# Weight blocks of the q and k projections placed 32 bytes apart, in eleven forms

## The chip, the cores and the metric

The kernel runs on one core of a Trainium2 chip. The metric is the device time of one execution in microseconds (us). The kernel before takes 675.37 us, the median of three runs (675.22, 675.37 and 675.39). A core has a matrix engine (TensorE, in the profile PE for its matmuls and PEld for its weight loads), a vector engine (VectorE, DVE), a scalar engine (ScalarE, ACT), a general engine (GpSimd, POOL) and a queue engine that issues DMAs (SyncE, SP).

## The reference: what is computed

A decoder trunk of two layers on 256 tokens of width 1024, everything in float32. Layer 0 mixes tokens with a forgetting attention of 16 heads of 64, layer 1 with a block attention that, at 256 tokens, is one causal block with a relative bias. After each mixer stands a SwiGLU of inner width 2816, and after it a gated embedding. Cut to what matters here:

```python
for i in range(DEPTH):                        # DEPTH = 2
    u = _rmsnorm(h, attn_norm_g[i])
    proj = u @ w_in[i]                        # 1024 x 3072: q, k and v
    q, k, v = heads(proj)                     # 16 heads of 64
    h = h + merge(attention_i(q, k, v)) @ w_o[i]
    u = _rmsnorm(h, ffn_norm_g[i])
    gu = u @ ffn_w_in[i]                      # 1024 x 5632
    h = h + (silu(gu[..., :D_FF]) * gu[..., D_FF:]) @ ffn_w_out[i]
    gate = sigmoid(_rmsnorm(h, ple_norm_g[i]) @ ple_w_gate[i])
    h = h + gate * (p[i] @ ple_w_up[i])
return _rmsnorm(h, final_norm_g)
```

## The kernel before, in words

**Weights.** All weights come as 216 *halves*, each 128 partitions by 1024 float32 columns (512 KB), in the order in which they are used. The function `half` takes the next one: SP issues its DMA into a buffer `raw`, ACT copies it, rounded, into a buffer `whi` (line 136), and DVE writes the difference of the two into `wlo` (line 137). There are six buffers each of `raw`, `whi` and `wlo`, so the three steps run ahead of the matmuls until a buffer that they need is still in use. The activations are split into a high and a low part in the same way (`nm.hi`, `nm.lo`), and every product is three matmuls (`mm3`, lines 82 to 84): high by high, high by low, low by high.

**Where a weight block lies.** The buffers are longer than the 1024 columns. `blocks` (which calls `half` with `at=APART`, 16 columns or 64 bytes) is used where the weights are the stationary operand of a matmul: each half is then eight blocks of 128 by 128, one for each step k of the sum over the width. `LINE` is 64 columns, 256 bytes. There is already one exception to an even placement: with `entry` (used for the first half of the SwiGLU's input weights that follows two output halves, and once for a half that comes after the matmuls of a norm), the low parts of the first two blocks begin 32 bytes (`FURTHER`, 8 columns) further than an even placement would have them, and the low parts of the other six 256 bytes further; DVE then writes `wlo` in two instructions (line 128), one of 256 and one of 768 columns. The high part stays in one piece, written by ACT at line 125.

**The attention stage.** First come eight halves for v, then sixteen for q and k. `project(j, a)` computes the queries (a = 0) or keys (a = 1) of the two heads of pair j: one half, eight blocks, 24 matmuls with 256 columns moving, into the tile `pq`. The work is written out in this order by hand, for j from 0 to 7:

```python
for j in range(NP):
    project(j, 0)
    if j >= 1:
        scores(j - 1)
    if j >= 2:
        transposes(j - 2)
    project(j, 1)
    if j >= 2:
        values(j - 2)
```

`scores` (tile `sp`) multiplies queries by keys and runs the softmax on DVE and ACT; it needs `qkt`, `qkh` and `qkl`, which DVE and ACT make from `pq` (lines 387 and 238). `transposes` (tile `pp`, line 429) turns the probabilities, `values` (tile `po`, lines 82 to 84 and 444) multiplies them by v. So from j = 2 on `project(j, 1)` follows transposes on TensorE, and from j = 3 on `project(j, 0)` follows values. `project(1, 1)` follows scores alone. The 24 matmuls of `project(2, 0)` come straight behind those of `project(1, 1)`.

What an engine executes is in one order that is fixed when the program is built, from the order in which the work is written and from when buffers come free; on each engine an instruction that waits holds up all that stand behind it. In a few places, therefore, the order on TensorE is not the written one: in layer 1 three matmuls of `project(3, 0)` stand among those of the first `values`.

**The other stages** that use `blocks` are the SwiGLU's input halves (tile `gu`, 24 matmuls each, as above). The output projection (`wo`), the SwiGLU's output (`fo`), v and the gate (`pg`) use the weights as the moving operand, 512 columns wide.

Of the kernel before, what the change touches and what calls it, by code (L numbers as in the profile page):

```python
# [28 lines left out]
F32R = mybir.dt.float32r  # L29
AF = mybir.ActivationFunctionType  # L30
ALU = mybir.AluOpType

P = 128
S = 256
D = 1024
KT = D // P
# [10 lines left out]
HW = 1024  # L47
# [7 lines left out]
LINE = 64  # L55
APART = 16
# [3 lines left out]
FURTHER = 8  # L60


@with_exitstack
def trunk(ctx: ExitStack, tc: tile.TileContext, x, xt, pt, w, wf, cst, gains, gf, bf, rel, hot, rvm, out):
    nc = tc.nc
    one = ctx.enter_context(tc.tile_pool(name="one", bufs=1))
    work = ctx.enter_context(tc.tile_pool(name="work", bufs=2))
# [4 lines left out]
    def bank(name):  # L72
        return ps.tile([P, 512], F32, tag="bank", name=name)

    def f32(ap):
        return ap.bitcast(F32)
# [3 lines left out]
    def mm3(o, a, b, start, stop):  # L80
        (ah, al), (bh, bl) = a, b
        mm(o, ah, bh, start=start, stop=False, skip_group_check=True)  # L82
        mm(o, ah, bl, start=False, stop=False, skip_group_check=True)  # L83
        mm(o, al, bh, start=False, stop=stop, skip_group_check=True)  # L84
# [26 lines left out]

    state = {"next": 0}

    def half(at=0, entry=0):


        i = state["next"]
        state["next"] += 1
        raw = work.tile([P, HW], F32, tag="raw", bufs=RAW, name=f"raw{i}")
        hi = work.tile([P, HW + LINE], F32R, tag="whi", bufs=6, name=f"whi{i}")[:, at:at + HW]  # L120
        lt = work.tile([P, HW + 2 * LINE], F32R, tag="wlo", bufs=6, name=f"wlo{i}")
        lo = lt[:, at:at + HW]
        if entry:
            nc.sync.dma_start(raw, w[i])
            nc.scalar.activation(hi, raw, AF.Copy)  # L125
            ats = [(at + FURTHER, 0, entry), (at + LINE, entry, HW)]
            for a, c0, c1 in ats:
                nc.vector.tensor_tensor(lt[:, a + c0:a + c1], raw[:, c0:c1], f32(hi[:, c0:c1]), op=ALU.subtract)  # L128
            return hi, [lt[:, a + k * P:a + (k + 1) * P] for a, c0, c1 in ats for k in range(c0 // P, c1 // P)]
        parts = 2 if i < 2 else 1  # L130
        for q in range(parts):
            c = slice(q * HW // parts, (q + 1) * HW // parts)
            if i == 0 and q == 1:
                nc.sync.dma_start(hx[:, 1], xt[:, 1])
            nc.sync.dma_start(raw[:, c], w[i][:, c])
            nc.scalar.activation(hi[:, c], raw[:, c], AF.Copy)  # L136
            nc.vector.tensor_tensor(lo[:, c], raw[:, c], f32(hi[:, c]), op=ALU.subtract)  # L137
        return hi, lo

    def blocks(entry=False):  # L140

        hi, lo = half(APART, ENTRY * P if entry else 0)
        hi = [hi[:, k * P:(k + 1) * P] for k in range(KT)]
        return hi, lo if entry else [lo[:, k * P:(k + 1) * P] for k in range(KT)]
# [54 lines left out]

    nm = Norm(0)  # L200
    first = [half()]
    nm.block(0, hx[:, 0])
    nm.block(1, hx[:, 1])
    first.append(half())
    for b in range(1, 4):
        nc.sync.dma_start(hx[:, 2 * b:2 * b + 2], xt[:, 2 * b:2 * b + 2])
# [14 lines left out]
    ht = work.tile([BUCKETS, RVW], F32, tag="e", bufs=3, name="ht")  # L221
# [14 lines left out]
    def split(hi, lo, src):  # L236
        nc.scalar.activation(hi, src, AF.Copy)  # L237
        nc.vector.tensor_tensor(lo, src, f32(hi), op=ALU.subtract)
# [86 lines left out]
    def attention(layer, nm, mid, early, nf):  # L325
        vb = [bank(f"v{layer}_{b}") for b in range(4)]
        rest = None
        for c in range(4):
            wt = [early.pop(0) if early else half() for _ in range(2)]
            for kk in range(2):  # L330
                hi, lo = wt[kk]
                k = 2 * c + kk
# [23 lines left out]
        for t in range(2):  # L356
            for hf in range(2):
                col = nm.col[:, t:t + 1]
                src = vb[2 * t + hf].rearrange("p (j s d) -> p j s d", s=2, d=DH)
                for s in range(2):  # L360
                    at = (slice(None), slice(4 * hf, 4 * hf + 4), slice(2 * s * DH, (2 * s + 1) * DH))
# [7 lines left out]
        o = work.tile([P, NP, 2, S], F32R, tag="act", name=f"o{layer}")  # L369
# [3 lines left out]
        pq = {}  # L373

        def project(j, a):
            hi, lo = blocks()
            if a == 0:
                pq[j] = bank(f"pq{layer}_{j}")
            bk = pq[j]
            for k in range(KT):  # L380
                mm3(bk[:, a * S:(a + 1) * S], (hi[k], lo[k]), nm.k(k),
                    start=(k == 0), stop=(k == KT - 1))
            if a == 0:
                return
            del pq[j]
            t = work.tile([P, 2, S], F32, tag="qkt", name=f"qkt{layer}_{j}")
            nc.vector.tensor_tensor(t.rearrange("p a s -> p (a s)"), bk,
                                    nm.row.rearrange("p a s -> p (a s)"), op=ALU.mult)
            th = work.tile([P, 2, S], F32R, tag="qkh", name=f"qkh{layer}_{j}")
            tl = work.tile([P, 2, S], F32R, tag="qkl", name=f"qkl{layer}_{j}")  # L390
            split(th, tl, t)
            qk[j] = t, th, tl
# [54 lines left out]
# [9 lines that stand above are left out]
            if layer == 0 and j >= 4:  # L456
                moba[0](j - 4)
# [23 lines left out]
    def ffn(layer, nm, filler, np_):  # L481
# [3 lines left out]
        def up(fs):  # L485

            bks = {f: bank(f"gu{layer}_{f}") for f in fs}

            def step(f, a, wt, k, start):
                mm3(bks[f][:, a * S:(a + 1) * S], (wt[0][k], wt[1][k]), nm.k(k), start, k == KT - 1)  # L490

            if fs[0] == 0:
                wts = {f: (blocks(), blocks()) for f in fs}
                for k in range(KT):
                    if k == 3:
                        nm.turn(1)
                        nm.square(1)
                    for f in fs:
                        for a in range(2):
                            step(f, a, wts[f][a], k, k == 0 and a == 0)  # L500
                nm.root()
                return fs, bks
            for a in range(2):
                wt = blocks(a == 1 if fs[0] == 2 else a == 0 and fs[0] % 2 == 0)
                for k in range(KT):
                    step(fs[0], a, wt, k, k == 0)
                if fs[0] == 2 and a == 0:
                    nm.spread()
                    gated(*early)
            gated(fs, bks)  # L510
# [154 lines left out]
    for layer in range(2):  # L665
# [5 lines left out]
        got = []  # L671
# [98 lines left out]
```

## Time and profile before

| | |
|---|---|
| median of three runs | 675.37 us |
| the profiled execution | 675.98 us, with a span of 674.2 us from its first to its last instruction |
| instructions | 11845 |
| PE busy | 658.9 us (98% of the span), 4604 matmuls |
| DVE busy | 455.1 us (67%) |
| ACT busy | 386.1 us (57%) |
| granted TensorE clock | 0.998 of full speed |

The profiled execution is thus 0.61 us longer than the median of the runs. In the profile's rows, L82 is line 82 of the kernel, `pq<-g,whi` says that tile `pq` is written from tiles `g` and `whi`; a group of like instructions has its busy time in us and the mean duration of one in ns, and then the idle time of the engine just before them with what ended it. In a list in order of time, the first column is the start in us from the span's start and the second the duration. Matmuls follow each other before the one before has ended, so the pace at which TensorE works is the distance between two starts, and not the duration of one.

### The profile page before, as it was taken

The numbers are of one execution on the slowest core, as the hardware profiler recorded it, in microseconds if no ns is written. First come the engines' busy times: TensorE is split into PE (matmuls) and PEld (weight loads), VectorE is DVE, ScalarE is ACT, GpSimd is POOL, SyncE is SP. The second block draws the span as 40 slices with busy tenths as digits, with TensorE's granted clock in tenths as the row PEclk, the third lists the DMA queues.
The fourth block names the chain that finished last, engine by engine and source line by source line (L and its number), as shares of the span: only waits on it lengthen the run. The fifth ranks groups of instructions, "written<-read, shape, count | busy, mean of one in ns | idle before, by whom it ended". The sixth has DMA issues, their size and how long they took to land.

```text
span 674.2 us, 11845 instructions
## 1 busy us (share of the span) xinstructions
PE 658.9 (98%) x4604; PEld 604.1 (90%) x4604; DVE 455.1 (67%) x802; ACT 386.1 (57%) x698; POOL 31.5 (5%) x57
## 2 busy tenths in 40 slices
PE   8999999999999999999999999999999999999994
PEld 6788998999999999998889999889999999999884
DVE  4699886676666666666676888765766666666673
ACT  6886665664444444547665766655544444444663
POOL 1067000000000000000000000000000000000000
PEclk9999999999999999999999999999999999999999
DMA  7979333456556655665585533343765655565401
GB/s 271 377 280 370 128 126 125 157 163 213 189 194 197 197 192 201 199 193 176 185 285 198 175 126 126 109 173 113 236 190 201 197 190 188 193 210 201 162 1 63
DMA packets 37529, 125.90 MB, mean 187 GB/s; under 512 B 4240, under 2 KB 7008, under 8 KB 37472
## 3 DMA queue, kind: packets, MB, share of 16 engines
q1 hardware_dynamic: 36016, 121.35, 53.4%
q0 software_dynamic: 608, 2.11, 0.9%
q10 hardware_dynamic: 848, 1.68, 0.7%
q8 instruction: 36, 0.59, 0.3%
q14 instruction: 21, 0.17, 0.1%
HBM read 124.03 MB, written 4.24 MB: 190 GB/s over the span
## 4 chain that ended last, share of the span: by engine, by line
PE 91%; DMA 3%; ACT 2%; DVE 2%; issue 1%; SPq 0%; POOLq 0%; ACTq 0%; DVEq 0%; POOL 0%
PE gu L84 12%; PE gu L82 12%; PE gu L83 12%; PE fo L82 6%; PE fo L83 6%; PE fo L84 6%; PE pq L82 4%; PE pq L84 4%; PE pq L83 4%; PE wo L82 2%; PE wo L84 2%; PE wo L83 2%; PE pg L82 2%; PE pg L84 2%; PE pg L83 2%; DMA raw<-w 2%
## 5 line engine op out<-in xcount | busy, mean ns | idle before, releaser
L137 DVE TENSOR_TENSOR wlo<-raw,whi 128x1024 fp32r<-128x1024 f32 (+1 forms) x198 | 240.8, 1219 | 137.7 <-ACT whi L136 137.5
L136 ACT ACTIVATE whi<-raw 128x1024 fp32r<-128x1024 f32 (+1 forms) x198 | 206.7, 1049 | 159.1 <-PE gu L83 48.2
L82 PE MATMUL gu<-g,whi 128*128 128x256 f32 x704 | 195.5, 278 | 0.0
L84 PE MATMUL gu<-g,wlo 128*128 128x256 f32 x704 | 195.1, 277 | 0.0
L83 PE MATMUL gu<-g,whi 128*128 128x256 f32 x704 | 195.1, 277 | 0.0
L82 PEld LDWEIGHTS gu<-g,whi 128*128 128x128 f32 x704 | 132.6, 188 | 0.8
L83 PEld LDWEIGHTS gu<-g,whi 128*128 128x128 f32 x704 | 132.2, 188 | 0.7
L84 PEld LDWEIGHTS gu<-g,wlo 128*128 128x128 f32 x704 | 132.1, 188 | 0.0
L82 PE MATMUL pq<-g,whi 128*128 128x256 f32 x256 | 73.8, 288 | 0.0
L84 PE MATMUL pq<-g,wlo 128*128 128x256 f32 x256 | 71.7, 280 | 0.0
L83 PE MATMUL pq<-g,whi 128*128 128x256 f32 x256 | 71.6, 280 | 0.0
L82 PE MATMUL fo<-whi,fh 128*128 128x512 f32 x176 | 68.9, 391 | 0.0
L83 PE MATMUL fo<-wlo,fh 128*128 128x512 f32 x176 | 68.7, 390 | 0.0
L84 PE MATMUL fo<-whi,fl 128*128 128x512 f32 x176 | 68.5, 389 | 0.0
L82 PEld LDWEIGHTS pq<-g,whi 128*128 128x128 f32 x256 | 48.1, 188 | 0.9 <-issue 0.6
L83 PEld LDWEIGHTS pq<-g,whi 128*128 128x128 f32 x256 | 48.6, 190 | 0.0
L84 PEld LDWEIGHTS pq<-g,wlo 128*128 128x128 f32 x256 | 48.4, 189 | 0.0
L237 ACT ACTIVATE fh<-sg 128x256 fp32r<-128x256 f32 x44 | 18.2, 416 | 48.6 <-DVE sg L519 48.6
L128 DVE TENSOR_TENSOR wlo<-raw,whi 128x256 fp32r<-128x256 f32 (+1 forms) x40 | 26.0, 688 | 22.5 <-ACT whi L125 22.5
L84 PEld LDWEIGHTS fo<-whi,fl 128*128 128x128 f32 x176 | 33.0, 188 | 7.0
L82 PEld LDWEIGHTS fo<-whi,fh 128*128 128x128 f32 x176 | 33.0, 188 | 6.2
L83 PEld LDWEIGHTS fo<-wlo,fh 128*128 128x128 f32 x176 | 33.0, 188 | 6.1
(139 smaller groups left out, 982.2 us busy)
## 6 DMA issues: line engine op xcount, KB each, us to landing
raw<-w SPq DMA_DIRECT2D x214, 512.0 KB, 4.1
d<-d SPq DMA_DIRECT2D x4, 768.0 KB, 12.8
bias<-cd POOLq DMA_DIRECT2D x4, 512.0 KB, 9.0
bias<-d SPq DMA_DIRECT2D x4, 512.0 KB, 5.2
raw<-w SPq DMA_DIRECT2D x4, 256.0 KB, 5.4
h<-x ACTq DMA_DIRECT2D x2, 512.0 KB, 5.3
hx<-xt SPq DMA_DIRECT2D x3, 256.0 KB, 5.4
p<-pt SPq DMA_DIRECT2D x2, 256.0 KB, 4.7
```

The costliest lines, as they stand in the source:

```text
L82: mm(o, ah, bh, start=start, stop=False, skip_group_check=True)
L83: mm(o, ah, bl, start=False, stop=False, skip_group_check=True)
L84: mm(o, al, bh, start=False, stop=stop, skip_group_check=True)
L128: nc.vector.tensor_tensor(lt[:, a + c0:a + c1], raw[:, c0:c1], f32(hi[:, c0:c1]), op=ALU.subtract)
L136: nc.scalar.activation(hi[:, c], raw[:, c], AF.Copy)
L137: nc.vector.tensor_tensor(lo[:, c], raw[:, c], f32(hi[:, c]), op=ALU.subtract)
L237: nc.scalar.activation(hi, src, AF.Copy)
```

## The change

A table `FORMS` gives 24 of the 32 q and k projections a form, by layer, by a and by j. A form says how many blocks at the front of the high part, and how many of the low part, begin 32 bytes off (`8` columns further, or with `-8` nearer), and in one form the whole high part lies 256 bytes further. Where the offset is positive, the other blocks of that part lie 256 bytes further than before; where it is negative, they stay. The eleven forms are: low 1, low 2, low 2 with the high part far, low 1 back, high 1, high 1 back, high 2, both 1, both 1 back, both 2, both 2 back.

- Low 2 at `project(1, 1)` of both layers.
- Layer 0, a = 1, j = 2 to 7: low 2, both 1 back, both 1, both 2, high 1, low 1.
- Layer 1, a = 1, j = 2 to 7: both 2 back, low 1 back, high 1 back, high 2, low 2 far, low 2.
- Layer 0, a = 0, j = 3 to 7: low 2, both 1 back, both 1, both 2, high 1.
- Layer 1, a = 0, j = 3 to 7: low 1, both 2 back, low 1 back, high 2, low 2 far.

A half with a form is made of more instructions: its low part always by two on DVE (the first one or two blocks, and the rest), and its high part by two on ACT where the high part is split (13 of the 24). The data, the matmuls and their order of writing are the same. The `whi` buffers grow from 1088 to 1152 columns (256 bytes each), and all that lies behind them in the memory moves by 1536 bytes.

```diff
--- before.py
+++ after.py
@@ -60,6 +60,20 @@
 FURTHER = 8
 
 
+_LO2, _BOTH1_BACK, _BOTH1, _BOTH2, _HI1, _LO1 = ((0, 0), (2, 8), 0), ((1, -8), (1, -8), 0), ((1, 8), (1, 8), 0), \
+    ((2, 8), (2, 8), 0), ((1, 8), (0, 0), 0), ((0, 0), (1, 8), 0)
+_BOTH2_BACK, _LO1_BACK, _HI1_BACK, _HI2, _LO2_FAR = ((2, -8), (2, -8), 0), ((0, 0), (1, -8), 0), ((1, -8), (0, 0), 0), \
+    ((2, 8), (0, 0), 0), ((0, 0), (2, 8), 64)
+FORMS = {(0, 1, 1): _LO2, (1, 1, 1): _LO2}
+for _l, _a, _j, _forms in (
+        (0, 1, 2, (_LO2, _BOTH1_BACK, _BOTH1, _BOTH2, _HI1, _LO1)),
+        (1, 1, 2, (_BOTH2_BACK, _LO1_BACK, _HI1_BACK, _HI2, _LO2_FAR, _LO2)),
+        (0, 0, 3, (_LO2, _BOTH1_BACK, _BOTH1, _BOTH2, _HI1)),
+        (1, 0, 3, (_LO1, _BOTH2_BACK, _LO1_BACK, _HI2, _LO2_FAR))):
+    for _n, _f in enumerate(_forms):
+        FORMS[_l, _a, _j + _n] = _f
+
+
 @with_exitstack
 def trunk(ctx: ExitStack, tc: tile.TileContext, x, xt, pt, w, wf, cst, gains, gf, bf, rel, hot, rvm, out):
     nc = tc.nc
@@ -111,15 +125,37 @@
 
     state = {"next": 0}
 
-    def half(at=0, entry=0):
+    def half(at=0, entry=0, form=None):
 
 
         i = state["next"]
         state["next"] += 1
         raw = work.tile([P, HW], F32, tag="raw", bufs=RAW, name=f"raw{i}")
-        hi = work.tile([P, HW + LINE], F32R, tag="whi", bufs=6, name=f"whi{i}")[:, at:at + HW]
+        ht = work.tile([P, HW + 2 * LINE], F32R, tag="whi", bufs=6, name=f"whi{i}")
+        hi = ht[:, at:at + HW]
         lt = work.tile([P, HW + 2 * LINE], F32R, tag="wlo", bufs=6, name=f"wlo{i}")
         lo = lt[:, at:at + HW]
+        if form:
+            nc.sync.dma_start(raw, w[i])
+            got = []
+            for t, (n, off), at in ((ht, form[0], at + form[2]), (lt, form[1], at)):
+                places = [(at + off, 0, n), (at + (LINE if off > 0 else 0), n, KT)]
+                for a, k0, k1 in places:
+                    if k0 == k1:
+                        continue
+                    o, c = t[:, a + k0 * P:a + k1 * P], slice(k0 * P, k1 * P)
+                    if t is ht:
+                        nc.scalar.activation(o, raw[:, c], AF.Copy)
+                    else:
+                        for b0, b1 in sorted({(max(k0, x), min(k1, y)) for x, y in ((0, form[0][0]), (form[0][0], KT))}):
+                            if b0 < b1:
+                                a0 = got[1][b0]
+                                nc.vector.tensor_tensor(t[:, a + b0 * P:a + b1 * P], raw[:, b0 * P:b1 * P],
+                                                        f32(ht[:, a0:a0 + (b1 - b0) * P]), op=ALU.subtract)
+                got.append([t[:, a + k * P:a + (k + 1) * P] for a, k0, k1 in places for k in range(k0, k1)])
+                if t is ht:
+                    got.append([a + k * P for a, k0, k1 in places for k in range(k0, k1)])
+            return got[0], got[2]
         if entry:
             nc.sync.dma_start(raw, w[i])
             nc.scalar.activation(hi, raw, AF.Copy)
@@ -137,8 +173,10 @@
             nc.vector.tensor_tensor(lo[:, c], raw[:, c], f32(hi[:, c]), op=ALU.subtract)
         return hi, lo
 
-    def blocks(entry=False):
-
+    def blocks(entry=False, form=None):
+
+        if form:
+            return half(APART, 0, form)
         hi, lo = half(APART, ENTRY * P if entry else 0)
         hi = [hi[:, k * P:(k + 1) * P] for k in range(KT)]
         return hi, lo if entry else [lo[:, k * P:(k + 1) * P] for k in range(KT)]
@@ -373,7 +411,7 @@
         pq = {}
 
         def project(j, a):
-            hi, lo = blocks()
+            hi, lo = blocks(form=FORMS.get((layer, a, j)))
             if a == 0:
                 pq[j] = bank(f"pq{layer}_{j}")
             bk = pq[j]
```

## The prediction

> **What bounds the kernel now.** I read the page first: busy times and the chain that ended last.
>
> ```profile
> PE 658.9 (98%) x4604; PEld 604.1 (90%) x4604; DVE 455.1 (67%) x802; ACT 386.1 (57%) x698; POOL 31.5 (5%) x57
> PE 91%; DMA 3%; ACT 2%; DVE 2%; issue 1%; SPq 0%; POOLq 0%; ACTq 0%; DVEq 0%; POOL 0%
> ```
>
> TensorE carries nine tenths of the chain. So the time moves only with the pace of its matmuls, or where it has to wait. The profiled execution took 675.98 us (span 674.2); the median of the runs is 675.37. I sum against the span and put the sum on the median.
>
> Second view: TensorE's instructions in order of time around the first `project(j, 1)` and `project(j, 0)` of a pair in the middle of layer 0, the wide stretch after `fo` in the SwiGLU, and `project(1, 1)` of layer 1.
>
> ```profile
> 79.44 0.36 PE L82 MATMUL pq<-g,whi 128*128 128x256 f32 x1
> 82.35 0.28 PE L82 MATMUL po<-th,vhi 128*128 128x256 f32 x1
> ...
> 83.42 0.36 PE L82 MATMUL pq<-g,whi 128*128 128x256 f32 x1
> 83.62 0.28 PE L83 MATMUL pq<-g,whi 128*128 128x256 f32 x1
> ...
> 86.21 0.28 PE L84 MATMUL pq<-g,wlo 128*128 128x256 f32 x1
> ...
> 157.79 0.28 PE L82 MATMUL gu<-g,whi 128*128 128x256 f32 x1
> ...
> 167.87 0.28 PE L84 MATMUL gu<-g,wlo 128*128 128x256 f32 x1
> ...
> 372.25 0.28 PE L83 MATMUL pq<-g,whi 128*128 128x256 f32 x1
> ...
> 377.67 0.28 PE L84 MATMUL pq<-g,wlo 128*128 128x256 f32 x1
> ```
>
> The same kind of matmul goes at two paces. From 83.62 to 86.21 stand matmuls 2 to 24 of a half: 2.59 us over 22 steps, 117.7 ns each. From 157.79 to 167.87 stand matmuls 7 to 96: 10.08 over 89, 113.3 ns. From 372.25 to 377.67 are 2 to 48: 5.42 over 46, 117.8 ns. The groups of these stretches tell the pace by the mean duration too (281 ns slow, 276 fast): first 54 to 101 us, then 385 to 425.6, then 45.8 to 51.1, then 158 to 167.
>
> ```profile
> L83 PE MATMUL pq<-g,whi 128*128 128x256 f32 x88 | 24.7, 281 | 0.0
> L83 PE MATMUL po<-tl,vhi 128*128 128x256 f32 x12 | 3.4, 281 | 0.0
> ...
> L83 PE MATMUL pq<-g,whi 128*128 128x256 f32 x77 | 21.6, 281 | 0.0
> ...
> L83 PE MATMUL pq<-g,whi 128*128 128x256 f32 x16 | 4.4, 276 | 0.0
> ...
> L83 PE MATMUL gu<-g,whi 128*128 128x256 f32 x27 | 7.5, 276 | 0.0
> ```
>
> So all halves that follow transposes or values run slow, and the values with them; `project(1, 1)` and `project(2, 0)` of layer 0 are fast already. A pace, once found, lasts until other work comes between. What the change can win is 4.4 ns (117.7 less 113.3) on the matmuls behind the place where a pace flips.
>
> **What the trace says of the 32 bytes.** Low 2 is in the kernel already. After `fo` it stands before a fast stretch; after the norm's `pr` it does not. And a half without any form can flip, at 384 us in layer 1:
>
> ```profile
> 157.07 0.28 PE L82 MATMUL gu<-g,whi 128*128 128x256 f32 x1
> 157.67 0.28 PE L84 MATMUL gu<-g,wlo 128*128 128x256 f32 x1
> ...
> L83 PE MATMUL gu<-g,whi 128*128 128x256 f32 x22 | 6.2, 281 | 0.0
> ...
> 384.16 0.28 PE L84 MATMUL pq<-g,wlo 128*128 128x256 f32 x1
> 384.52 0.28 PE L84 MATMUL pq<-g,wlo 128*128 128x256 f32 x1
> ...
> L83 PE MATMUL gu<-g,whi 128*128 128x256 f32 x12 | 3.4, 281 | 0.0
> ```
>
> The two rows of 157 us are matmuls 1 and 6: five steps in 0.60 us, 120 ns each, slower than either pace, and then it is fast. So a flip costs some 12 to 15 ns at first (five steps of 117.7 are 0.589). The group with 22 is of 143.1 to 151 us, after `pr`, with low 2: still slow. The rows of 384 us are three steps in 0.36, 120 ns each, without a form. The last group, of 127.7 to 131.8 us, is the SwiGLU's first 36 matmuls, after `wo` and without a form: slow. I read this as two stable rhythms between weight load and matmul, and a small delay at the right moment moves TensorE from one to the other. Low 2 gave it after 512-wide work and not after 128-wide work. Transposes and the end of values are 128-wide like `pr`, so I give low forms one in four. Forms that move the high part touch the second load of the half already and two loads of three; no row shows one, so their share is bounded by none and all, and I take one half, nearest to the mixed outcomes above (one kind of place flips, one doesn't).
>
> **What a flip is worth.** In a half after transposes: 18 of 24 steps at 4.4 ns, less 15 ns, 0.065 us, and the six values matmuls of 256 columns behind it 0.026: 0.09. After values: 0.065 (scores follow, which change little). `project(1, 1)` of layer 1 with `project(2, 0)` behind it: 42 steps, less 15 ns, 0.17. The half at 384 us, `project(3, 0)` of layer 1, is fast and can only lose its 0.07. So 11 places at 0.09, 10 at 0.065 and one at 0.17: 1.81 us if all flip, nothing if none. Of the 21, 13 move the high part (half: 6.5) and 8 only the low (a quarter: 2). That is 8.5 at a mean of 0.078, 0.66, and a quarter of 0.17, 0.04: together -0.70 us.
>
> **What it costs on DVE and ACT.** Every form writes its low part in two instructions, 13 write the high part in two.
>
> ```profile
> L137 DVE TENSOR_TENSOR wlo<-raw,whi 128x1024 fp32r<-128x1024 f32 x194 | 238.1, 1230 | 130.7 <-ACT whi L136 130.5
> L128 DVE TENSOR_TENSOR wlo<-raw,whi 128x768 fp32r<-128x768 f32 x20 | 19.0, 951 | 0.0
> L128 DVE TENSOR_TENSOR wlo<-raw,whi 128x256 fp32r<-128x256 f32 x20 | 8.5, 424 | 22.5 <-ACT whi L125 22.5
> L136 ACT ACTIVATE whi<-raw 128x1024 fp32r<-128x1024 f32 x194 | 204.3, 1057 | 155.4 <-PE gu L83 48.2 <-issue 41.6 <-PE pq L83 21.1
> L136 ACT ACTIVATE whi<-raw 128x512 fp32r<-128x512 f32 x4 | 2.4, 623 | 3.7 <-DMA raw<-w 3.7
> ```
>
> Low split: 424 + 951 - 1230 = 0.145 us more on DVE. High split: twice 623 less 1057, 0.19 on ACT. In the middle of the stage this is covered: DVE works 39.72 of the 47 us from 54 to 101 (row below), and those 47 us hold 11 halves (88 matmuls of line 83, 8 in each): 11 splits are 1.6 us where 7.3 are idle. If that cover were gone, 24 splits would cost 3.5 us. It is gone at the start of layer 0:
>
> ```profile
> 40.19:53.10 12.91, 12.77 (x24) 1.00 0.96 371
> 54.00:101.00 47.00, 39.72 (x124) 1.00 0.54 193
> PE sp L402 <- DVE qkl L238: 2.2, 2, 1.3
> 39.08 2.97 ACT L136 ACTIVATE whi<-raw 128x1024 fp32r<-128x1024 f32 x3
> 42.47 0.68 DVE L387 TENSOR_TENSOR qkt<-pq,row 128x512 f32<-128x512 f32 x1
> 43.07 1.22 DVE L137 TENSOR_TENSOR wlo<-raw,whi 128x1024 fp32r<-128x1024 f32 x1
> 44.20 0.95 DVE L238 TENSOR_TENSOR qkl<-qkt,qkh 128x512 fp32r<-128x512 f32 x1
> 52.17 0.94 DVE L238 TENSOR_TENSOR qkl<-qkt,qkh 128x512 fp32r<-128x512 f32 x1
> 60.13 0.94 DVE L238 TENSOR_TENSOR qkl<-qkt,qkh 128x512 fp32r<-128x512 f32 x1
> 61.55 0.20 PEld L402 LDWEIGHTS sp<-qkl,qkh 64*128 64x128 f32 x2
> 369.68 1.23 DVE L137 TENSOR_TENSOR wlo<-raw,whi 128x1024 fp32r<-128x1024 f32 x1 [0.34 <-ACT whi L136]
> 370.82 0.68 DVE L238 TENSOR_TENSOR qkl<-qkt,qkh 128x512 fp32r<-128x512 f32 x1
> 371.58 0.20 PEld L402 LDWEIGHTS sp<-qkl,qkh 64*128 64x128 f32 x2
> ```
>
> From 40.19 to 53.10 DVE is busy 12.77 of 12.91 us, and TensorE waits twice for its `qkl`, the first two scores. Between 40.19 and the first `qkl` DVE makes three lows that get a form (the last at 43.07), between it and the second two more. Each has 0.145 more: the first wait ends 0.43 later, the second another 0.29, 0.72 us in all. ACT's added piece (the third of these lows has a split high) delays nothing: the three copies before it end at 42.05, 0.19 later would be 42.24, and DVE turns to that low at 43.07. From below the price is nothing (should the pieces fall in gaps), from above a whole small instruction of 424 ns for each of five, 2.1 us; I take 0.145, since the rows are of this very split. In layer 1 `qkl` ends at 371.50 and its weight load starts at 371.58, with one split low ahead of it that DVE waits for anyhow: 0.145 less 0.08, 0.07 us. The third `qkl` of layer 0 ends at 61.07 and its weights are loaded at 61.55, so half a microsecond covers the two splits before it.
>
> The SP queue issues the same DMAs. The buffers behind `whi` move by 1536 bytes, a multiple of 256, as the even placements before all are: nothing.
>
> **The sum.** -0.70 + 0.72 + 0.07 = +0.09 us: 675.5 us, a share of 0.01%. About 0.2%, 1.35 us, is what a measurement of this kernel can tell from no change.
>
> **The rivals.**
> 1. *The offsets do nothing to TensorE after transposes and values.* The stretch after `pr` speaks for it, the one after `fo` against. Then only the cost is left: 675.37 + 0.79 = 676.2 us. [...]
> 2. *Nearly all flip*: 675.37 + 0.79 - 1.81 = 674.4 us, and 673.6 with the start hidden. For it speaks that a small delay was enough at 384 us; against it, low 2 after `pr`.
> 3. *Slower*: the order on DVE is fixed anew with the added instructions, and one whole low of 1.23 us is put ahead of one of the two first `qkl`. TensorE waits that much longer: 675.5 + 1.23 = 676.7 us. It decides from the first low that is put there on, as DVE has only 0.14 us idle in that stretch; against it speaks that the order of writing is the same.
>
> **How the numbers follow.** Forecast (a good third flips) 0.53; rival 1 0.20; rival 2 0.13; rival 3 0.14. The likeliest case alone spans 674.9 to 676.1 (flips between one in five and three in five, and a split price 0.1 to 0.2). With the rivals, 674.3 to 676.7. Slower by over 0.2% is rival 3's upper half with small mishaps beside it, 0.13; faster by over 0.2% needs nearly all flips and no price at the start, 0.08; the rest, 0.79, is within.
>
> **What would show it.** Groups of `pq` between 54 and 101 and between 385 and 425 us with a mean between 276 and 281 ns, half by half 281 or 276; lows in two pieces whose sum is 1.375 us; `sp` waiting for `qkl` 2.9 us in place of 2.2. I am wrong if nearly all halves go at one pace, if TensorE waits for DVE in other places, or if the SwiGLU's stretches change pace.

## The result, and the profile after

The changed kernel takes 674.31 us (median of 17 runs) against 675.39 us beside it: the ratio is 0.9982, with a 95% interval of 0.9974 to 0.999. That is 0.18% faster, 1.1 us. I had forecast no change, 0.01% slower. The profiled execution took 674.07 us with a span of 672.2 us, 2.0 us less than the profiled span before; 0.8 us of it is that the profiled execution before lay 0.6 us above its median (675.98 to 675.39) and this one 0.2 below (674.07 to 674.31).

The page after, in the lines that answer to those shown: the matmuls are as many as before, DVE has 24 instructions more (802 to 826), ACT 13 (698 to 711).

```profile
span 672.2 us, 11882 instructions
PE 658.2 (98%) x4604; PEld 603.4 (90%) x4604; DVE 456.5 (68%) x826; ACT 388.7 (58%) x711; POOL 29.6 (4%) x57
PE 95%; DVE 2%; ACT 1%; DMA 1%; issue 1%; POOLq 0%; SPq 0%; DVEq 0%; POOL 0%; ACTq 0%
```

The halves of q and k, groups by line in seven windows (each row is line 97, the old line 83, in the steady part of one half; 281 ns is slow, 276 fast). In this order: low 2 (54.4 to 56.9 us), both 1 back (62.8 to 65.3), both 1 (71.4 to 73.5), both 2 (79.5 to 81.8), high 1 (87.9 to 90.1), low 1 (96.2 to 98.3), and low 2 again, in layer 1 (420.7 to 422.9).

```profile
L97 PE MATMUL pq<-g,whi 128*128 128x256 f32 x8 | 2.2, 281 | 0.0
...
L97 PE MATMUL pq<-g,whi 128*128 128x256 f32 x8 | 2.2, 281 | 0.0
...
L97 PE MATMUL pq<-g,whi 128*128 128x256 f32 x7 | 1.9, 276 | 0.0
...
L97 PE MATMUL pq<-g,whi 128*128 128x256 f32 x7 | 2.0, 281 | 0.0
...
L97 PE MATMUL pq<-g,whi 128*128 128x256 f32 x7 | 1.9, 276 | 0.0
...
L97 PE MATMUL pq<-g,whi 128*128 128x256 f32 x7 | 1.9, 276 | 0.0
...
L97 PE MATMUL pq<-g,whi 128*128 128x256 f32 x7 | 1.9, 276 | 0.0
```

So some forms flip a half (it goes from the slow pace to the fast one) and some don't; by the starts of the matmuls 13 of the 21 slow halves are fast now, and `project(3, 0)` of layer 1, the one that was fast, is slow. The two kinds of beginning, in order of time: a half with high 1, which flips, and one with both 2, which doesn't.

```profile
87.59 0.28 PE L97 MATMUL pq<-g,whi 128*128 128x256 f32 x1
88.06 0.28 PE L98 MATMUL pq<-g,wlo 128*128 128x256 f32 x1
88.28 0.28 PE L97 MATMUL pq<-g,whi 128*128 128x256 f32 x1
...
79.19 0.28 PE L97 MATMUL pq<-g,whi 128*128 128x256 f32 x1
79.67 0.28 PE L98 MATMUL pq<-g,wlo 128*128 128x256 f32 x1
79.90 0.28 PE L97 MATMUL pq<-g,whi 128*128 128x256 f32 x1
```

The rows are matmuls 2, 6 and 8. High 1 takes 0.47 us for the four steps to matmul 6 and then 0.11 a step; both 2 takes 0.48 and then 0.115, and stays there.

What I had not counted stands in the SwiGLU. Its stretches to which the change gives nothing new, after (127.4 to 131, 143.1 to 150.4, 457.2 to 466.1 and 467.2 to 474.7 us), and the last two of them before (458.2 to 467.8, 468.5 to 476.7); before, the first two are the slow groups that the prediction quotes:

```profile
L97 PE MATMUL gu<-g,whi 128*128 128x256 f32 x11 | 3.0, 276 | 0.0
...
L97 PE MATMUL gu<-g,whi 128*128 128x256 f32 x22 | 6.1, 276 | 0.0
...
L97 PE MATMUL gu<-g,whi 128*128 128x256 f32 x27 | 7.5, 276 | 0.0
...
L97 PE MATMUL gu<-g,whi 128*128 128x256 f32 x23 | 6.4, 276 | 0.0
```

```profile
L83 PE MATMUL gu<-g,whi 128*128 128x256 f32 x28 | 7.9, 281 | 0.0
...
L83 PE MATMUL gu<-g,whi 128*128 128x256 f32 x24 | 6.7, 281 | 0.0
```

From first matmul to the next stage these four were 4.25, 8.57, 9.98 and 8.57 us and are 4.10, 8.28, 9.62 and 8.28. That is 1.08 us, more than half of the 2.0 us between the two profiles. The rest, by the same starts: q, k and their values -1.17 us from flips, +0.04 in `project(1, 1)` of layer 0, which low 2 had slow for its first matmuls, +0.37 from a new order in layer 1 (below), and -0.19 before the first `pq`, where the weights of the first halves land.

The two waits at the start of layer 0, which I had priced at 0.72 us more, are as they were (the waits between 40 and 58 us: sum, count and longest):

```profile
PE sp L440 <- DVE qkl L276: 2.1, 2, 1.4
```

DVE ahead of the first of them, in order of time (start, length):

```profile
39.95 2.50 DVE L153 TENSOR_TENSOR wlo<-raw,whi 128x256 fp32r<-128x256 f32 x4 [0.72 <-ACT whi L148]
42.97 1.28 DVE L153 TENSOR_TENSOR wlo<-raw,whi 128x128 fp32r<-128x128 f32 x2
44.17 0.69 DVE L276 TENSOR_TENSOR qkl<-qkt,qkh 128x512 fp32r<-128x512 f32 x1
```

The two lows in four pieces take 2.50 us and the third, in two, 1.28, where a low in one piece took 1.22 (row of 43.07 before). So a split costs 0.06 to 0.07 us and not 0.145: in this stretch each of these instructions begins 0.08 us before the one ahead of it has ended (the third low ends at 44.25 us and `qkl` begins at 44.17), which the sum of the durations leaves out. And the first `qkl` took 0.69 us in place of 0.95, which is not the change's doing: in all sixteen profiles a `qkl` takes 0.94 or 0.95 us where GpSimd adds a mask at the same time and 0.68 or 0.69 where it doesn't (5 and 27 of the 32 `qkl` in the first profiles of the two kernels), and only in the first profile of the kernel before did GpSimd begin early enough (at 43.91 us; after, at 45.83). In the second profile of that kernel, `e2_before` below, the first `qkl` took 0.68 us as well.

The new order: in layer 1 a second group of values is broken up. Its matmuls stand still once, and three of the next half come between.

```profile
398.35 0.28 PE L96 MATMUL po<-th,vhi 128*128 128x256 f32 x1
398.47 0.38 PE L97 MATMUL po<-tl,vhi 128*128 128x256 f32 x1
398.69 0.28 PE L98 MATMUL po<-th,vlo 128*128 128x256 f32 x1
398.80 0.38 PE L482 MATMUL po<-tf,vf 128*128 128x128 f32 x2
398.94 0.36 PE L96 MATMUL pq<-g,whi 128*128 128x256 f32 x1
...
399.38 0.35 PE L482 MATMUL po<-tf,vf 128*128 128x128 f32 x1
```

From 398.47 to 398.69 is 0.22 us where 0.12 is usual, and the change back and forth costs another 0.1. Together with the values of `project(3, 0)`, which were broken up before and are worse so now, 0.37 us.

### The profile page after: what moved, and what is told of

Same layout as the page of the kernel before. It is cut to its first block, busy times and chain, and to the rows that moved or that the text cites. A ratio compares the mean times of both kernels' runs of the same rounds, so it can differ in the third digit from the quotient of the medians.

```text
span 672.2 us, 11882 instructions
## 1 busy us (share of the span) xinstructions
PE 658.2 (98%) x4604; PEld 603.4 (90%) x4604; DVE 456.5 (68%) x826; ACT 388.7 (58%) x711; POOL 29.6 (4%) x57
## 3 DMA queue, kind: packets, MB, share of 16 engines
HBM read 124.03 MB, written 4.24 MB: 191 GB/s over the span
## 4 chain that ended last, share of the span: by engine, by line
PE 95%; DVE 2%; ACT 1%; DMA 1%; issue 1%; POOLq 0%; SPq 0%; DVEq 0%; POOL 0%; ACTq 0%
PE gu L98 12%; PE gu L96 12%; PE gu L97 12%; PE fo L96 6%; PE fo L97 6%; PE fo L98 6%; PE pq L96 4%; PE pq L97 4%; PE pq L98 4%; PE v L96 2%; PE wo L96 2%; PE wo L98 2%; PE wo L97 2%; PE v L97 2%; PE v L98 2%; PE pg L96 2%
## 5 line engine op out<-in xcount | busy, mean ns | idle before, releaser
L173 DVE TENSOR_TENSOR wlo<-raw,whi 128x1024 fp32r<-128x1024 f32 (+1 forms) x174 | 210.3, 1212 | 124.6 <-ACT whi L172 119.8
L172 ACT ACTIVATE whi<-raw 128x1024 fp32r<-128x1024 f32 (+1 forms) x174 | 182.0, 1049 | 142.7 <-PE gu L97 47.1
L97 PE MATMUL pq<-g,whi 128*128 128x256 f32 x256 | 71.4, 279 | 0.0
L153 DVE TENSOR_TENSOR wlo<-raw,whi 128x256 fp32r<-128x256 f32 (+3 forms) x48 | 33.4, 723 | 9.6 <-ACT whi L148 9.6
```

What stands on the lines that cost most here:

```text
L153: nc.vector.tensor_tensor(t[:, a + b0 * P:a + b1 * P], raw[:, b0 * P:b1 * P], f32(ht[:, a0:a0 + (b1 - b0) * P]), op=ALU.subtract)
```

## The experiments

Three theories of where the 1.08 us in the SwiGLU came from, and of what a form does: (1) the 32-byte offsets set the pace, on the spot or by a moment that is carried on; (2) the moved buffers do; (3) chance. In each layer the SwiGLU begins with three stretches of matmuls, named here by their number: 36 behind the output projection, 84 behind the transposes (`tp`) of the norm and 72 behind its `pr`.

### The two kernels again, the wide buffers alone, the pieces alone

`e1_again` and `e2_before` are the two kernels unchanged.

> The changed kernel once more, to see which changes of pace come back. If the paces are set by where the blocks lie (theory 1) or by where the buffers lie (theory 2), every q, k and SwiGLU stretch goes at the pace that it had in the first profile: 674.3 us, the SwiGLU's first 36 matmuls of layer 0 in 4.10 us, the 72 after its norm in 8.28, in layer 1 the 84 in 9.62 and the 72 in 8.28. If the SwiGLU's stretches flip by chance (theory 3), some of these four come back at 4.25, 8.57, 9.98 and 8.57.

> The kernel before once more. Theories 1 and 2: all four SwiGLU stretches without a reset slow again (4.25, 8.57, 9.98, 8.57 us), all q and k halves after transposes and values slow, 675.4 us. Theory 3: some of the four are fast this time, and the time moves by 0.15 to 0.36 us for each.

`e3_wide` against the kernel before:

```diff
-        hi = work.tile([P, HW + LINE], F32R, tag="whi", bufs=6, name=f"whi{i}")[:, at:at + HW]
+        hi = work.tile([P, HW + 2 * LINE], F32R, tag="whi", bufs=6, name=f"whi{i}")[:, at:at + HW]
```

> The kernel before with only the whi buffers widened to 1152 columns, no form. Theory 2 (moving the buffers by 256 bytes each made the SwiGLU's stretches fast): these four win 1.08 us, 674.3 us. Theory 1 and my prediction (moves by multiples of 256 bytes do nothing): 675.4 us and the same paces as before. Theory 3: anything between for these four, nothing for q and k.

`e4_split` against the changed kernel:

```diff
-            for t, (n, off), at in ((ht, form[0], at + form[2]), (lt, form[1], at)):
-                places = [(at + off, 0, n), (at + (LINE if off > 0 else 0), n, KT)]
+            for t, (n, off), at in ((ht, form[0], at), (lt, form[1], at)):
+                places = [(at, 0, n), (at, n, KT)]
```

> The changed kernel with every piece written as there, but all offsets zero, so that each half lies evenly: the added instructions and the wide buffers alone. By my prediction's cost 676.2 us; by the profile after, where a split costs 0.06 and not 0.145 us on DVE, 675.4 to 675.6. Theory 1: all q and k halves after transposes and values slow, SwiGLU as before. Theory 3: some SwiGLU stretches fast although no block is moved.

Ratios to the kernel before: again 0.9973 (0.9963 to 0.9983), the kernel before itself 1.0001 (0.9988 to 1.0014), wide 0.9996 (0.9986 to 1.0006), split 1.0006 (0.9997 to 1.0015). What these stretches took, from start to start in the traces, in us, with the runs of the later sections that leave the SwiGLU's own forms as they were (the 84 of layer 0 took 9.98 in all of these):

| kernel | 36, layer 0 | 72, layer 0 | 36, layer 1 | 84, layer 1 | 72, layer 1 |
|---|---|---|---|---|---|
| before, e2_before, e3_wide, e4_split, e8_one_lo1, e10_all_hi2 (each) | 4.25 | 8.57 | 4.25 | 9.98 | 8.57 |
| after | 4.10 | 8.28 | 4.24 | 9.62 | 8.28 |
| e1_again | 4.10 | 8.28 | 4.10 | 9.98 | 8.28 |
| e5_all_hi1, e11_all_whole (each) | 4.10 | 8.28 | 4.10 | 9.98 | 8.28 |
| e6_all_lo1 | 4.25 | 8.57 | 4.24 | 9.62 | 8.28 |
| e7_all_both1, e9_hi1_layer1 (each) | 4.25 | 8.57 | 4.10 | 9.98 | 8.28 |

Theory 2 falls: wide buffers change neither a pace of the SwiGLU nor the time. The added instructions alone cost at most 0.15%, and flip none of the 21 halves; their trace has the new order of the values in layer 1 too (at 398.8 us), so the pieces bring that order and not the offsets. Chance is no part of the SwiGLU where no form stands ahead of it: in all ten such layers of the table (both layers of before, e2, e3 and e4, layer 1 of e8, layer 0 of e9) every stretch is slow. Of the 15 layers with forms at all places after transposes and values, eleven have fast stretches and four have none (layer 0 of e6 and e7, both of e10). With the offsets the outcome is not quite the same each time either: of the two profiles of the changed kernel, one has layer 1's 84 fast and one its 36. The 72 are fast exactly where the 36 or the 84 are.

So the offsets in q and k did it, from a distance: theory 1 with a moment that is carried on, through the output projection. It can be seen there, in matmuls that the change doesn't touch: from the last six of `wo` to the SwiGLU's first are 1.47 us in every layer of the table whose 36 are fast, 1.45 in the two whose 84 are, and 1.46 in all others. It is not the pace of q and k that is carried: in layer 0 of e7 nine of the eleven halves are fast and the SwiGLU is slow, and in e11 no half with a form goes at the fast pace and the SwiGLU does. Which few nanoseconds decide, and where they arise, stays open.

A few halves of q and k do change from one execution to the next. `project(1, 1)` and `project(2, 0)` of layer 0, fast in the first profile of the kernel before, as the prediction read them, are slow in `e2_before`, which is the same kernel. In the two profiles of the changed kernel 20 of the 21 halves agree, with 13 and 12 fast.

### One form at all places

`e5_all_hi1` against the changed kernel (`e6_all_lo1` and `e7_all_both1` have `_LO1` and `_BOTH1` in the place of `_HI1`):

```diff
-FORMS = {(0, 1, 1): _LO2, (1, 1, 1): _LO2}
...
+FORMS = {(_l, _a, _j): _HI1 for _l in range(2) for _a, _j0 in ((1, 2), (0, 3)) for _j in range(_j0, 8)}
```

> High 1 at all 22 halves that follow transposes or values, and no form at the two behind scores. Theory 1a (what a form does hangs on the form: high 1 flipped both places where it stood): all 22 fast, each half 0.08 shorter and each values behind it 0.03, 2.1 us in all, and some of the SwiGLU's stretches with them: 672.4 to 673.6 us. Theory 1b (it hangs on the moment at which TensorE comes there, so each place has its own form): only a part fast, in layer 1 above all, where it hadn't stood, 673.8 to 674.8 us.

> Low 1 at all 22. My prediction gave low forms one place in four: 675 us. Theory 1a: low 1 was fast in layer 0 after transposes and slow in layer 1 after values, so perhaps all 11 after transposes, 1.2 us less, 674 to 674.5 us. Theory 1b: a mixture within each kind of place.

> Both 1 at all 22. Theory 1a: it flipped both places where it stood (after transposes and after values, layer 0), so all 22 fast, 672.4 to 673.6 us. Theory 1b: a mixture, 673.8 to 674.8 us. If the displaced blocks themselves cost anything, this one shows it against high 1 and low 1, as it moves three loads of 24.

High 1: 672.61 us, ratio 0.9952 (0.9934 to 0.9969). Both 1: 672.95 us, 0.9948 (0.9932 to 0.9964). Low 1: 676.38 us, 1.0008 (0.9994 to 1.0021). With high 1, 21 of the 22 halves are fast; the one that is slow is `project(3, 0)` of layer 1, of which five matmuls stand among the first values. Groups of 62 to 101 and of 386 to 425 us, with the values in them:

```profile
L90 PE MATMUL pq<-g,whi 128*128 128x256 f32 x72 | 19.9, 277 | 0.0
L90 PE MATMUL po<-tl,vhi 128*128 128x256 f32 x10 | 2.8, 276 | 0.0
...
L90 PE MATMUL pq<-g,whi 128*128 128x256 f32 x72 | 19.9, 277 | 0.0
L90 PE MATMUL po<-tl,vhi 128*128 128x256 f32 x10 | 2.8, 276 | 0.0
```

So with one high block it hangs on the form and hardly on the place (theory 1a). Both 1 flips all but three: the two halves at 54 and 58 us, and again `project(3, 0)` of layer 1. Low 1 flips 18 of 22, and is none the faster for it: there the added pieces led to another order in five pairs, as at 398 us above. One of them, in order of time:

```profile
75.67 0.28 PE L89 MATMUL po<-th,vhi 128*128 128x256 f32 x1
76.06 0.39 PE L90 MATMUL po<-tl,vhi 128*128 128x256 f32 x1
76.28 0.28 PE L91 MATMUL po<-th,vlo 128*128 128x256 f32 x1
76.40 0.38 PE L475 MATMUL po<-tf,vf 128*128 128x128 f32 x2
76.54 0.37 PE L89 MATMUL pq<-g,whi 128*128 128x256 f32 x1
...
76.98 0.38 PE L475 MATMUL po<-tf,vf 128*128 128x128 f32 x2
```

The step from 75.67 to 76.06 is 0.39 us where 0.11 is usual, the next 0.22. What the halves won, the values gave back. Layer 0's SwiGLU is fast with high 1 and slow with the other two (table above), though most halves are fast in all three.

### What is carried over

The table of forms in `e8_one_lo1`, and then in `e9_hi1_layer1`, against `e5_all_hi1`:

```diff
+FORMS = {(0, 1, 7): _LO1}
...
+FORMS = {(_l, _a, _j): _HI1 for _l in (1,) for _a, _j0 in ((1, 2), (0, 3)) for _j in range(_j0, 8)}
```

> Low 1 at the last half of layer 0 alone, project(7, 1), all else as before the change. If the SwiGLU's stretches of layer 0 changed pace because the moment at which TensorE came to them had been moved by the halves ahead (carried over), this one form can already do it: the 36 matmuls in 4.10 and the 72 in 8.28 us, about 0.55 us less in all with its own half. If it takes the forms of earlier halves too, only the own half and its values are shorter, by 0.07 and 0.03, and the SwiGLU stays at 4.25 and 8.57.

> High 1 at the 11 halves of layer 1 alone. If a changed pace in the SwiGLU is carried over from the attention of the same layer, layer 0's 36 and 72 matmuls stay at 4.25 and 8.57 us and layer 1's 72 go in 8.28 as in the other kernels with forms there; q and k of layer 1 win about 1.1 us: 674.1 to 674.6 us. If the moment is carried over the whole run, or the SwiGLU's pace is chance, layer 0's stretches change too, or layer 1's don't.

Low 1 at the last half of layer 0 alone: 675.69 us, ratio 0.9993 (0.9983 to 1.0004). The half is fast, the SwiGLU slow in every stretch. One form at the end isn't enough. High 1 in layer 1 alone: 674.21 us, 0.9979 (0.9969 to 0.9989); the SwiGLU of layer 0 is slow and that of layer 1 fast in two of three stretches (table above). So a layer's own forms are enough for its SwiGLU. Whether forms in layer 0 reach layer 1 as well, no run shows.

### One block, two blocks, all blocks

The table in `e10_all_hi2` (two blocks of high 32 bytes further), and then in `e11_all_whole` (all blocks of both parts 32 bytes further, with nothing split):

```diff
+FORMS = {(_l, _a, _j): _HI2 for _l in range(2) for _a, _j0 in ((1, 2), (0, 3)) for _j in range(_j0, 8)}
...
+FORMS = {(_l, _a, _j): ((8, 8), (8, 8), 0) for _l in range(2) for _a, _j0 in ((1, 2), (0, 3)) for _j in range(_j0, 8)}
```

> High 2 at all 22, against high 1 at all 22 (672.61 us). In the changed kernel the forms of one block flipped 8 of 11 halves and those of two 4 to 5 of 10. If the second displaced block takes back what the first gave (theory 2b), at most half of the halves are fast, 673.8 to 675 us; if one and two blocks are alike (theory 2a), 672.4 to 673.4 us.

> All eight blocks of high and of low 32 bytes further at the 22, so that no block lies unevenly to its neighbours within a half and nothing is split. If it is the step from a displaced block to an even one that gives the delay, nothing flips: 675.4 to 675.7 us, all 22 slow. If a displaced block's own load is what takes longer, all 24 loads do, and the halves are slower than before or fast at once: then the pace is neither 117.7 nor 113.3 ns, or the first of them flips it.

High 2: 674.9 us, 0.9984 (0.997 to 0.9998). After transposes it leaves the half slow, after values it flips it, in all pairs but the first of layer 0 (where it is the other way round). Groups of 70.9 to 73 and of 66.9 to 68.6 us:

```profile
L90 PE MATMUL pq<-g,whi 128*128 128x256 f32 x7 | 2.0, 282 | 0.0
...
L90 PE MATMUL pq<-g,whi 128*128 128x256 f32 x6 | 1.7, 276 | 0.0
```

Ten of the 22 are fast, and the time lies in the range of theory 2b. But two blocks are not simply worse than one: the second takes back what the first gave after transposes, and not after values. All blocks displaced: 675.6 us, 0.9995 (0.9983 to 1.0006). From 2nd to 24th matmul of a half after values:

```profile
76.35 0.28 PE L90 MATMUL pq<-g,whi 128*128 128x256 f32 x1
...
78.96 0.28 PE L91 MATMUL pq<-g,wlo 128*128 128x256 f32 x1
```

2.61 us over 22 steps, 118.6 ns: not fast, and slower than the even blocks' 117.7. Twelve halves settle at this pace (118.5 ns without their beginning), nine at 117.3, and one falls into the low clock of the last section. None comes to 113.3, so displacement alone doesn't free the fast pace; whether a displaced block costs anything by itself, two new paces on both sides of 117.7 don't tell. With the split halves beside it, it is the change from a displaced to an even block that goes with the fast pace, though high 2 after transposes shows that the change isn't always enough. It fits what this run did elsewhere: several values behind such halves, which read even blocks, and the 36 and 72 matmuls of the SwiGLU in both layers are fast.

### On the spot in the SwiGLU

`e13_best2` against `e5_all_hi1`. In the first half of the SwiGLU the high blocks 0 to 2 are even, block 3 lies 32 bytes further and blocks 4 to 7 lie 256 bytes further; the half behind the norm gets high 1 in place of its own form:

```diff
+                if t is ht and form[2] == "two":
+                    places = [(at, 0, 3), (at + 8, 3, 4), (at + LINE, 4, KT)]
...
-                wts = {f: (blocks(), blocks()) for f in fs}
+                wts = {f: (blocks(form=((0, 0), (0, 0), "two") if f == 0 else None), blocks()) for f in fs}
...
-                wt = blocks(a == 1 if fs[0] == 2 else a == 0 and fs[0] % 2 == 0)
+                wt = blocks(a == 0 and fs[0] % 2 == 0 and fs[0] > 2, form=_HI1 if fs[0] == 2 and a == 1 else None)
```

`e14_ffn_only` is the same with no form in q and k; `e12_best` moves block 0 of the first half too and adds a form at `project(1, 1)` of layer 1:

```diff
+FORMS = {}
...
+FORMS[1, 1, 1] = _HI1
...
-                    places = [(at, 0, 3), (at + 8, 3, 4), (at + LINE, 4, KT)]
+                    places = [(at + 8, 0, 1), (at + LINE, 1, 3), (at + LINE + 8, 3, 4), (at + 2 * LINE, 4, KT)]
```

> High 1 at the 22, at project(1, 1) of layer 1, and in the SwiGLU: high 1 in place of low 2 behind the norm, and in its very first half block 0 and block 3 (the first behind the second pair of transposes) of the high part 32 bytes further. If a displaced first high block flips the pace wherever it stands, the three stretches of each layer go in 4.10, 9.62 and 8.28 us whatever came before: against high 1 alone (672.61) another 0.36 in layer 0, 0.5 in layer 1 and 0.2 for project(1, 1), 671.4 to 671.8 us. If the stretches hang on what is carried over, no gain beyond project(1, 1).

> High 1 at the 22, and in the SwiGLU block 3 of the first high half displaced and high 1 in place of low 2 behind the norm; block 0 of the first half lies evenly. If the first 36 matmuls are carried over from the attention and were spoilt by their own displaced block in the run before, they go in 4.10 us now, the 84 in 9.63 and the 72 in 8.27 in both layers: against high 1 in the attention alone 0.7 us less, 671.9 us. If not, 4.25 us and 672.2 us.

> The same two forms in the SwiGLU and none in the attention. If a step on the spot sets the pace, the 84 go in 9.63 and the 72 in 8.27 us in both layers, with the 36 slow (4.25) and all q and k halves slow: about 1.2 us less than before, 674.2 us. If the carried moment is needed as well, the 84 and the 72 stay at 9.98 and 8.57.

Without any form in q and k (e14): 674.38 us, 0.9978 (0.9968 to 0.9989). Groups of 134 to 142 and of 459 to 467 us:

```profile
L90 PE MATMUL gu<-g,whi 128*128 128x256 f32 x23 | 6.3, 276 | 0.0
...
L90 PE MATMUL gu<-g,whi 128*128 128x256 f32 x23 | 6.4, 276 | 0.0
```

The 84 matmuls take 9.63 us and the 72 8.27 in both layers, whatever comes before: a step on the spot sets the pace (no run has the pieces at these two spots without the offset; in q and k such pieces flipped nothing). Block 3 is the first that is loaded behind the second pair of transposes. With high 1 in q and k as well (e13) 672.46 us, 0.9951 (0.9934 to 0.9969), with block 0 and `project(1, 1)` too (e12) 672.67 us, 0.9956 (0.9942 to 0.9971): by their traces the 84 and 72 are fast, the first 36 are slow in both (4.25 us), and `project(1, 1)` of layer 1 stays slow under high 1. The three versions with high 1 can't be told apart by their times; each beats both kernels. Why the 36 are fast after e5 and slow after e13, which differ ahead of them in no form but in the making of the weights, stays open; the traces differ already in the output projection, where the last six matmuls take 1.47 us in e5 and 1.46 in e13.

## Why the prediction was wrong

*The two paces.* Right. 117.7 and 113.3 ns came back in every run, and a pace mostly lasts until other work comes between (behind the beginning of high 1 at 87 us, after, 18 steps of 113 or 114 ns). Of the delay only a part is shown: that half has two steps of 120 and 122 ns ahead of its fast pace, but the one with both 2 at 79 us has 119 and 123 and stays slow. That the paces are rhythms between weight load and matmul was my reading of the rows; why there are two, no run shows.

*How many flip, and what a flip is worth.* The sum was right by luck. I had taken 8.5 of 21 and -0.70 us; 13 flipped, -1.17 us, of which the new order of the values in layer 1 took 0.37 and the first matmuls of `project(1, 1)` 0.04, so -0.76 us is left. The mis-sized term is the low forms' share: of the 8 low ones 6 flipped where I had counted 2, of the 13 high ones 7 where I had counted 6.5. Low 1 flips 18 of 22 (e6), and with a displaced second block it depends on the place (e10). The places were miscounted by one, at little cost: 12 stand after transposes and 9 after values, not 11 and 10. And the pace of `project(1, 1)`, which I took from one profile, is another in the next. The trace before showed only low 2, so it could not tell this. I took the failure of low 2 behind `pr` for one of 128-wide work in general; high 1 at the same spot flips.

*The cost on DVE.* The step that failed first: +0.72 us at the start of layer 0 and 0.07 in layer 1. The waits there are 2.1 us after 2.2, and over all profiles 1.7 to 2.2 without pieces in that stretch and 1.6 to 2.2 with them. A split costs 0.06 to 0.07 us, as the durations that I added overlap by 0.08. The pieces alone (e4) cost 0.4 us at the most likely, between nothing and 1; some 0.3 of it are, by its trace, the new order of the values in layer 1, which my sum had at nothing.

*What I costed at nothing.* The step that failed most: the stretches that the change leaves alone. -1.08 us in the SwiGLU is the largest term of the difference. The prediction named this as a sign of its being wrong, and gave it no term. It could have given it a bound: the rows suggested that the pace of a stretch hangs on a few ns at its start, and so that changed halves ahead of it may change it.

*The moved buffers.* Right: e3 moves them and nothing follows (ratio 0.9996).

*The rivals.* The time came out at rival 2's (674.4), by luck: not nearly all flipped, and the SwiGLU made up for it. Of rival 3 the new order came true, though not ahead of `qkl` and not with its time: two groups of values in layer 1, and in e6 it cost what the flips won. Rival 1 falls. One high block of eight 32 bytes off at 22 halves changes the time by 0.48% (e5, 672.61 us), and the pieces alone give none of it (e4, ratio 1.0006). So for these float32 matmuls with a new weight for each 256 columns the pace does depend on where a block lies; by what way, no run shows.

## What to carry to other kernels

Where every matmul has its own weight load, look at the distance between starts and not at busy time: here like matmuls had two steady paces 4% apart (117.7 and 113.3 ns a step), while PE was busy 98% of the span before and after. One displaced weight block ahead of even ones, in the high part, freed the fast pace in 21 of 22 halves after transposes or values (e5), and after scores it did not (e12); test such a form at all places at once, since a survey with another form at each place mixes the forms with the places and with what is carried over. And look for what the added pieces do to the fixed order of the other engines: it can take back the whole gain (e6, ratio 1.0008 with 18 of 22 halves flipped).

## What the runs showed that I had not expected

In three of the sixteen profiles a stretch at a lower clock follows a wait for `qkl` at the start of layer 0. Busy time of TensorE in three stretches of e2_before, the kernel before, and then of the first profile of the same kernel (columns: stretch, its length, PE busy and instructions, granted clock, DMA share, GB/s):

```profile
50.00:54.00 4.00, 2.32 (x19) 0.87 1.02 406
54.00:58.00 4.00, 4.00 (x26) 0.70 1.02 381
58.00:101.00 43.00, 43.00 (x381) 1.00 0.51 172
```

```profile
50.00:54.00 4.00, 2.72 (x26) 1.00 1.02 416
54.00:58.00 4.00, 4.00 (x37) 1.00 1.01 380
```

In one execution the granted clock is 0.87 and then 0.70 in the 8 us around its one wait, and full again behind them; from 54 to 58 us 26 matmuls go where 37 went; the spans of the two are 675.2 and 674.2 us. Two more of the profiles showed it (e6, 0.90 and 0.67; e11, 0.96 and 0.61). Matmul by matmul it is a stretch at little more than half the pace, 213 ns a step, and then the usual pace again (e2_before):

```profile
54.60 0.41 PE L83 MATMUL pq<-g,whi 128*128 128x256 f32 x1
54.81 0.41 PE L84 MATMUL pq<-g,wlo 128*128 128x256 f32 x1
...
56.48 0.28 PE L83 MATMUL pq<-g,whi 128*128 128x256 f32 x1
56.59 0.28 PE L84 MATMUL pq<-g,wlo 128*128 128x256 f32 x1
```

By the starts the low pace lasts 3.3 to 3.4 us in each of the three profiles, some 16 steps that take 95 ns more each: about 1.5 us, an estimate from these steps. The length of the wait alone doesn't decide it. The waits for `qkl` in e2_before and, without the drop, in e13_best2 (sum, count, longest):

```profile
PE sp L402 <- DVE qkl L238: 1.7, 1, 1.7
```

```profile
PE sp L436 <- DVE qkl L272: 1.7, 1, 1.7
```

What decides stays open. A lower clock goes with the scatter of all runs, 674.7 to 678.8 us for the kernel before: of its 117 executions in the experiments, the 32 with a mean granted clock of 0.992 or less all took 676.2 us or more, and the 25 with 0.996 or more at most 676.0. It is one reason why differences of a few tenths of a us between versions can't be read from their medians.
